# A down projection on two halves of TensorE's array, in a two-layer encoder trunk

## The chip, the cores and the metric

The kernel runs on one core of a Trainium2 chip. A core has TensorE (a 128 x 128 matrix array), VectorE (DVE in the profile), ScalarE (ACT), GpSimd (POOL) and SyncE (SP), which here mostly issues transfers. Matmul results go to eight banks of PSUM, each 128 partitions x 512 float32 values; all other data lie in SBUF, also 128 partitions. The metric is the device time of one execution in microseconds.

## The reference

The input is 512 tokens of width 1024 and 256 memory tokens. Two layers follow each other. Layer 0 mixes tokens by differential attention, layer 1 by chunked gated linear attention; both add a cross-attention into the memory tokens in parallel. After the mixer each layer has a gated MLP with a causal convolution of width 3:

```python
def conv_ffn(h, w_up, conv_w, conv_b, w_down):
    u = h @ w_up                       # 1024 -> 2 x 2816
    c = depthwise_causal_conv(u) + conv_b
    a, g = jnp.split(c, 2, axis=-1)
    return (jax.nn.silu(g) * a) @ w_down   # 2816 -> 1024

for i in range(2):
    h = rms_norm(x, attn_norm[i])
    ...
    x = x + jnp.concatenate([mix, cross], axis=-1) @ w_out[i]
    h = rms_norm(x, ffn_norm[i])
    x = x + conv_ffn(h, w_up[i], conv_w[i], conv_b[i], w_down[i])
```

The case is about the last product, `@ w_down`, in both layers: for each of the 1024 outputs a sum over 2816 hidden values, for 512 tokens.

## The kernel before, in words

The residual stream is held transposed: `xT[k]` holds 128 of the 1024 features on the partitions and the 512 tokens along the free dimension. Every large product is done in three terms to keep float32 precision: each operand is split into a rounded part (`hi`) and the rest (`lo`), both of the rounded type float32r, and hi x hi, hi x lo and lo x hi are summed in PSUM. The function `product` (lines 345 to 352) does this for one output tile: for each 128-feature tile of the input it issues three matmuls (lines 350, 351, 352) whose weights are a 128 x 128 block and whose moving operand is 512 tokens wide. Each matmul is preceded by its own load of weights (PEld in the profile). The projections of the mixers use `gemm` (lines 316 to 342, matmuls at 329 to 331), also in three terms, with the tokens as weights.

The MLP (`ffn`, lines 1113 to 1195) works in two halves of the hidden width, of 6 and 5 blocks of 256. In each half the up products come first, 4 per block, with banks tagged "mm" and "sm" in turn (line 1123); VectorE and ScalarE do the convolution, the gate and the split of the result into `mids`, one pair (hi, lo) for each 128 hidden features, 12 or 10 of them. Then comes the down projection of that half: for each of four pieces of 256 outputs, two banks, "lg" and "tp", take one output tile of 128 each; `product` sums over all `mids`, and `update` (line 1075) adds the bank to `xT` on VectorE. There are two banks of each of the four tags, so that a piece can begin while the piece before is still being added. In the second half of layer 0 `update` also makes the split operands of the next layer (line 310 on VectorE) and the running sum of squares (lines 421 to 426), and the stream is saved to DRAM; in the second half of layer 1 each finished tile goes to the output. The very last tile is added and sent in two halves of 256 tokens, by the queues of SyncE and ScalarE (lines 1185 to 1187).

TensorE's order is the order of the program, written by hand. Weights come in blocks of 128 x 1024 by SyncE's queue, ahead of use; ScalarE rounds each block to `whi` (line 252), VectorE takes the rest to `wlo` (line 255). Behind the down projection of layer 0 stands layer 1's first projection, `gemm` with 272 columns: two of its token blocks take "mm" banks and two "lg" banks, the operands made from the last tiles are used last, and after the first block TensorE sums the squares (line 430).

The attention parts already use matmuls on 64 partitions in plain float32: the logits of differential attention (line 736) and of the memory attention (line 608) alternate between partitions 0 to 63 and 64 to 127, each half with a bank of its own. The memory attention's values (line 646) alternate between two halves of the array's columns.

Of the kernel before, what the change touches and what calls it, by code (L numbers as in the profile page):

```python
# [178 lines left out]
def trunk(ctx, tc, head_d, x_t, mem_t, wpack, cols_a_d, cols_d, conv_d, gate_d, rel_bias, diff_lambda, consts, onehot, out):  # L179
    nc = tc.nc  # L180
    mm = nc.tensor.matmul
    V, A, G = nc.vector, nc.scalar, nc.gpsimd
# [9 lines left out]
    def bank(tag):  # L192
        return ps.tile([128, 512], F32, name=f"ps_{tag}", tag=tag)

    def xtile():
        return xs.tile([128, S], F32, name="xt", tag="xs", bufs=XS)

    def split_tiles(pool=None, tag="xs", bufs=XS):
        pool = pool or xs
        return (pool.tile([128, S], F32R, name=tag + "h", tag=tag, bufs=bufs),  # L200
                pool.tile([128, S], F32R, name=tag + "l", tag=tag, bufs=bufs))
# [4 lines left out]
    def blk(b, w=128):  # L206
        return slice(w * b, w * b + w)
# [13 lines left out]
    def tables(name):  # L221
        tc.keep_in_program_order(A.preload_act_table_set(name))


    def newton(v, y, t):
        V.tensor_mul(t, y, y)
        V.scalar_tensor_tensor(t, t, -0.5, v, op0=ALU.mult, op1=ALU.mult)
        V.scalar_tensor_tensor(y, t, 1.5, y, op0=ALU.add, op1=ALU.mult)
# [65 lines left out]
    def weights(key, by_block=False):  # L294
        i = used[0]
        assert plan[i][0] == key, (plan[i][0], key)
        limit = first_of[i] + WB if by_block else first_of[min(i + 2, len(plan))]
        while done[0] < min(max(limit, first_of[i + 1]), len(order)):
            make_block()
        used[0] += 1  # L300
        parts, made[i] = made[i], None
        return parts
# [5 lines left out]
    def split(hi, lo, src, gain):  # L308
        A.activation(hi, src, AF.Copy, scale=gain)
        V.scalar_tensor_tensor(lo, src, gain, hi.bitcast(F32), op0=ALU.mult, op1=ALU.subtract)  # L310
# [34 lines left out]
    def product(p, parts, n, pairs, ids=None):  # L345
        ids = range(len(parts)) if ids is None else ids
        first, last = (ids[0], ids[-1]) if len(ids) == len(parts) else (0, len(parts) - 1)
        for i in ids:
            (hi, lo), (bh, bl) = parts[i], pairs[i]
            mm(p, hi[:, blk(n)], bh, start=i == first, stop=False)  # L350
            mm(p, hi[:, blk(n)], bl, start=False, stop=False)  # L351
            mm(p, lo[:, blk(n)], bh, start=False, stop=i == last)  # L352


    xT = [None] * KT
# [12 lines left out]
    def col(i, t=cols):  # L368
        return t[:, i:i + 1]

    c_attn = lambda l, k: col(8 * l + k, cols_a)
# [27 lines left out]
    def bias_rows(rs, oh):  # L399
        out = []  # L400
        for tag, c in (("lg", slice(0, 512)), ("tp", slice(512, 640))):
            p = bank(tag)[:, :c.stop - c.start]
            mm(p, rs, oh[:, c], start=True, stop=True)
            out.append(p[:6])
        return out
# [12 lines left out]
    first = [bank("mm"), bank("mm"), bank("sm"), bank("sm")]  # L418

    def squares(src, acc):  # L420
        sq = xtile()
        A.activation(sq, src, AF.Square)
        if acc[0] is not None:
            V.tensor_add(sq, sq, acc[0])
        acc[0] = sq
# [17 lines left out]
    with tc.tile_pool(name="ini", bufs=1) as ip, tc.manual_schedule(engines={E.Activation, E.DVE, E.Pool, E.SP}):  # L443
# [10 lines left out]
        p = bank("tp")  # L454
        for n in (4, 2):
            mm(p[:, :128 * n].rearrange("p (a b) -> p a b", a=n), idle, idle.unsqueeze(1).to_broadcast([128, n, 128]),
               start=True, stop=True)
# [23 lines left out]
        parts, acc, split_w = [], [None], [None]  # L481
# [22 lines left out]
        for k in range(KT):  # L504
# [6 lines left out]
            if k == 5:  # L511
                rows = bias_rows(rs, oh)
# [9 lines left out]
            hi, lo = parts[k]  # L522
# [6 lines left out]
            for b, i, t in todo:  # L529
                xp, w = terms[i]  # L530
                mm(first[b][:, t], xp[:, blk(b)], w[:, t], start=k == 0 and i == 0 and t is not right,
                   stop=k == KT - 1 and i == 2)
# [542 lines left out]
    def update(n, p, gain, acc):  # L1075
        V.tensor_add(xT[n], xT[n], p)
        if gain is None:
            return
        xh[n], xl[n] = split_tiles()
        split(xh[n], xl[n], xT[n], gain(n))  # L1080
        squares(xT[n], acc)
# [31 lines left out]
    def ffn(pool, l, acc):  # L1113
        rB = pool.tile([128, S], F32, name="rB", bufs=1)
        us = [pool.tile([128, S + 128], F32, name=f"u{i}", bufs=1)[:, :S + 2] for i in range(4)]
        for u in us:
            G.memset(u[:, 0:2], 0.0)
        nu = [0]

        def up(parts, n):  # L1120
            i = nu[0]
            nu[0] += 1
            p = bank("mm" if i % 4 < 2 else "sm")
            product(p, parts, n, list(zip(xh, xl)))
            return p, us[i % 4]

        def conv(p, u, j):
            V.tensor_mul(u[:, 2:], p, rB)  # L1128
            c = pool.tile([128, S], F32, name="cvo", bufs=6)
            A.activation(c, u[:, 2:], AF.Identity, scale=cv[l][:, 2, j:j + 1], bias=cv[l][:, 3, j:j + 1])  # L1130
            V.scalar_tensor_tensor(c, u[:, 1:S + 1], cv[l][:, 1, j:j + 1], c, op0=ALU.mult, op1=ALU.add)  # L1131
            V.scalar_tensor_tensor(c, u[:, 0:S], cv[l][:, 0, j:j + 1], c, op0=ALU.mult, op1=ALU.add)
            return c

        def row_scales(sq):
            p = bank("tp")
            (one, _), (hi, lo) = split_tiles(), split_tiles()
            G.memset(one[:, :128].bitcast(F32), 1.0)
            A.copy(hi, sq)
            V.tensor_sub(lo, sq, hi.bitcast(F32))  # L1140
            mm(p, one[:, :128], hi, start=True, stop=False)
            mm(p, one[:, :128], lo, start=False, stop=True)
            v, t = xtile(), xtile()
            A.activation(rB, p, AF.Ln, scale=1.0 / D, bias=eps)
            V.tensor_scalar(v, p, 1.0 / D, EPS, op0=ALU.mult, op1=ALU.add)
            A.activation(rB, rB, AF.Exp, scale=-0.5)
            newton(v, rB, t)

        base = 0
        for half, nq in enumerate(HALVES):  # L1150
            mids = []
            for q in range(base, base + nq):
                wa = weights(("ua", l, q))
                wg = None
                for n in range(2):
                    ua = up(wa, n)
                    wg = wg or weights(("ug", l, q))
                    ug = up(wg, n)
                    if q == 0 and n == 0:
                        row_scales(acc[0])  # L1160
                    ca = conv(*ua, 2 * q + n)
                    cg = conv(*ug, 22 + 2 * q + n)
                    A.activation(cg, cg, AF.Silu)
                    V.tensor_mul(ca, ca, cg)
                    mh, ml = split_tiles() if len(mids) < 5 else split_tiles(pool, "mid", 18)
                    A.copy(mh, ca)
                    V.tensor_sub(ml, ca, mh.bitcast(F32))
                    mids.append((mh, ml))
            last = half == 1
            if last and l == 0:  # L1170
                tables("natural_log_exp_and_others")
            acc2 = [None]
            for c in range(4):
                if last and l == 0 and c == 0:
                    gw = gate_raw[0] = pool.tile([128, S], F32, name="cvo", bufs=6)[:96, :384]
                    G.memset(gw, 0.0)
                    for b in range(3):
                        load(gw[32 * b:32 * b + 17], gate_d)
                pn = bank("lg"), bank("tp")
                parts = weights(("dn", l, base, c))  # L1180
                for n in range(2):
                    product(pn[n], parts, n, mids)
                for n in range(2):
                    if last and l == 1 and c == 3 and n == 1:
                        for t, queue in ((blk(0, S // 2), nc.sync), (blk(1, S // 2), nc.scalar)):
                            V.tensor_add(xT[7][:, t], xT[7][:, t], pn[n][:, t])
                            queue.dma_start(out[7, :, t], xT[7][:, t])
                        continue
                    update(2 * c + n, pn[n], (lambda k: c_attn(1, k)) if last and l == 0 else None, acc2)
                    if last and l == 0:  # L1190
                        nc.sync.dma_start(xres[2 * c + n], xT[2 * c + n])
                    if last and l == 1:
                        nc.sync.dma_start(out[2 * c + n], xT[2 * c + n])
            base += nq
        return acc2
# [87 lines left out]
```

## Time and profile before

| | |
|---|---|
| median of 3 runs | 1165.82 us (1165.61 to 1165.84) |
| the profiled execution's own time | 1165.97 us |
| its span, first to last instruction | 1164.1 us |
| TensorE busy, matmuls | 1159.3 us, 5656 matmuls |
| TensorE busy, loads of weights | 966.6 us, 5656 loads |
| VectorE busy | 750.9 us, 1259 instructions |
| ScalarE busy | 545.5 us, 951 instructions |
| the four stretches of the down projection | 65.28, 54.42, 65.28 and 54.42 us |

In a line of the timeline stand the start in microseconds, the duration, the engine, the line of the kernel and the operation, then output <- inputs, the weights' shape (rows * columns of the array), the moving operand's shape and the count of merged instructions; square brackets give idle time before it and what ended it. In the view of groups by line the last numbers are busy time, mean duration in ns and idle time before. In the view of one line or tile the three numbers are the least, median and longest duration in ns, then the first and last start. In the windows view a line is a stretch with its length and each engine's busy time in it (and count of instructions), the granted clock, the share of the transfer engines' time and GB/s. Matmuls overlap each other: the time from start to start tells their rate, the duration doesn't.

### The profile page before, as it was taken

What the parts mean: (1) busy time and instruction counts of PE and PEld (TensorE: products, weight loads), DVE (VectorE), ACT (ScalarE), POOL (GpSimd) and SP (SyncE); (2) the same over time, 40 slices, a digit from 0 to 9 for tenths busy, and PEclk for the clock granted to TensorE, in tenths of its full rate; (3) what the DMA queues carried; (4) which work ended last, traced back from release to release, by engine and by line L of the source; (5) the groups of instructions that cost most, each with busy time, mean ns of one, the idle gap of its engine ahead of it and who ended that gap; (6) DMA issues with size and microseconds to landing.
All of it is one profiled execution on the core that took longest, in us unless ns stands there. A gap on an engine that the chain in (4) does not pass through costs nothing.

```text
span 1164.1 us, 14796 instructions
## 1 busy us (share of the span) xinstructions
PE 1159.3 (100%) x5656; PEld 966.6 (83%) x5656; DVE 750.9 (64%) x1259; ACT 545.5 (47%) x951; POOL 6.5 (1%) x30
## 2 busy tenths in 40 slices
PE   9999999999999999999999999999999999999998
PEld 7888887888888888888888888988888888888887
DVE  7576778688677326677457637767976733576741
ACT  7676687555344213444337634436543421344420
POOL 0000000000000000000000000000000000000000
PEclk9999999999999999999999999999999999999999
DMA  8422242223223223222341220333332323231221
GB/s 298 162 81 85 77 140 73 72 102 130 76 91 125 83 84 125 73 95 98 121 145 60 99 100 7 114 118 104 105 112 73 108 92 109 90 110 73 91 100 45
DMA packets 39652, 117.76 MB, mean 101 GB/s; under 512 B 4767, under 2 KB 7256, under 8 KB 39582
## 3 DMA queue, kind: packets, MB, share of 16 engines
q1 hardware_dynamic: 39150, 116.44, 29.0%
q8 instruction: 44, 0.72, 0.2%
q10 hardware_dynamic: 432, 0.39, 0.1%
q14 instruction: 26, 0.21, 0.1%
HBM read 112.60 MB, written 4.21 MB: 100 GB/s over the span
## 4 chain that ended last, share of the span: by engine, by line
PE 99%; DMA 0%; ACT 0%; DVE 0%; DVEq 0%; issue 0%
PE ps_mm L350 9%; PE ps_mm L352 9%; PE ps_mm L351 9%; PE ps_sm L352 8%; PE ps_sm L350 8%; PE ps_sm L351 8%; PE ps_mm L329 6%; PE ps_mm L331 6%; PE ps_mm L330 6%; PE ps_tp L352 3%; PE ps_lg L352 3%; PE ps_lg L351 3%; PE ps_tp L351 3%; PE ps_lg L350 3%; PE ps_tp L350 3%; PE ps_tp L219 3%
## 5 line engine op out<-in xcount | busy, mean ns | idle before, releaser
L252 ACT CAST whi<-raw 128x1024 fp32r<-128x1024 f32 (+4 forms) x212 | 207.6, 986 | 247.1 <-PE ps_tp L351 120.9
L255 DVE TENSOR_TENSOR wlo<-raw,whi 128x1024 fp32r<-128x1024 f32 (+4 forms) x212 | 240.4, 1140 | 121.8 <-ACT whi L252 118.6
L350 PE MATMUL ps_mm<-xsh,whi 128*128 128x512 f32 x438 | 171.6, 392 | 0.0
L351 PE MATMUL ps_mm<-xsl,whi 128*128 128x512 f32 x438 | 170.5, 389 | 0.0
L352 PE MATMUL ps_mm<-xsh,wlo 128*128 128x512 f32 x438 | 170.5, 389 | 0.0
L350 PE MATMUL ps_sm<-xsh,whi 128*128 128x512 f32 x378 | 147.0, 389 | 0.0
L351 PE MATMUL ps_sm<-xsl,whi 128*128 128x512 f32 x378 | 147.0, 389 | 0.0
L352 PE MATMUL ps_sm<-xsh,wlo 128*128 128x512 f32 x378 | 147.0, 389 | 0.0
L329 PE MATMUL ps_mm<-whi,xsh 128*128 128x512 f32 (+2 forms) x328 | 126.5, 386 | 0.0
L1130 ACT ACTIVATE cvo<-u,cv 128x512 f32<-128x512 f32 x88 | 71.4, 815 | 112.1 <-DVE u L1128 112.1
L331 PE MATMUL ps_mm<-whi,xsl 128*128 128x512 f32 (+2 forms) x328 | 123.0, 375 | 0.0
L330 PE MATMUL ps_mm<-wlo,xsh 128*128 128x512 f32 (+2 forms) x328 | 122.8, 374 | 0.0
L351 PEld LDWEIGHTS ps_mm<-xsl,whi 128*128 128x128 f32 x438 | 82.3, 188 | 17.2 <-DVE xsl L310 0.4
L352 PEld LDWEIGHTS ps_mm<-xsh,wlo 128*128 128x128 f32 x438 | 82.2, 188 | 17.1
L350 PEld LDWEIGHTS ps_mm<-xsh,whi 128*128 128x128 f32 x438 | 82.2, 188 | 16.9 <-issue 0.3
L1131 DVE SCALAR_TENSOR_TENSOR cvo<-u,cv,cvo 128x512 f32<-128x512 f32 x88 | 65.7, 749 | 36.2 <-ACT cvo L1130 36.0
L351 PEld LDWEIGHTS ps_sm<-xsl,whi 128*128 128x128 f32 x378 | 70.9, 188 | 14.8
L352 PEld LDWEIGHTS ps_sm<-xsh,wlo 128*128 128x128 f32 x378 | 70.9, 188 | 14.7
L350 PEld LDWEIGHTS ps_sm<-xsh,whi 128*128 128x128 f32 x378 | 71.0, 188 | 14.7
L331 PEld LDWEIGHTS ps_mm<-whi,xsl 128*128 128x128 f32 x328 | 61.7, 188 | 11.4
L329 PEld LDWEIGHTS ps_mm<-whi,xsh 128*128 128x128 f32 x328 | 61.7, 188 | 11.0 <-issue 0.7
L330 PEld LDWEIGHTS ps_mm<-wlo,xsh 128*128 128x128 f32 x328 | 61.8, 188 | 10.0
(312 smaller groups left out, 1778.1 us busy)
## 6 DMA issues: line engine op xcount, KB each, us to landing
raw<-in_wpack_dram SPq DMA_DIRECT2D x178, 512.0 KB, 3.5
xt<-in_x_t_dram SPq DMA_DIRECT2D x15, 256.0 KB, 5.4
raw<-in_wpack_dram SPq DMA_DIRECT2D x15, 256.0 KB, 5.1
raw<-in_wpack_dram SPq DMA_DIRECT2D x8, 384.0 KB, 3.4
xres<-xt SPq DMA_DIRECT2D x8, 256.0 KB, 3.6
xt<-xres SPq DMA_DIRECT2D x8, 256.0 KB, 5.4
out_dram<-xt SPq DMA_DIRECT2D x7, 256.0 KB, 2.0
bt<-bias_d SPq DMA_DIRECT2D x6, 256.0 KB, 4.7
```

The costliest lines, as they stand in the source:

```text
L219: nc.tensor.transpose(dst, src, ident[:n, :n])
L252: ins = A.copy(hi[:, c], raw[:, c])
L255: V.tensor_sub(lo[:, c], raw[:, c], hi[:, c].bitcast(F32))
L329: mm(p, sh[k][:, blk(b)], hi, start=k == 0, stop=False)
L330: mm(p, sh[k][:, blk(b)], lo, start=False, stop=False)
L331: mm(p, sl[k][:, blk(b)], hi, start=False, stop=k == KT - 1)
L350: mm(p, hi[:, blk(n)], bh, start=i == first, stop=False)
L351: mm(p, hi[:, blk(n)], bl, start=False, stop=False)
L352: mm(p, lo[:, blk(n)], bh, start=False, stop=i == last)
L1130: A.activation(c, u[:, 2:], AF.Identity, scale=cv[l][:, 2, j:j + 1], bias=cv[l][:, 3, j:j + 1])
L1131: V.scalar_tensor_tensor(c, u[:, 1:S + 1], cv[l][:, 1, j:j + 1], c, op0=ALU.mult, op1=ALU.add)
```

## The change

A second function, `product_rows`, takes the place of `product` in the down projection alone. It takes two banks and, for each matmul that `product` would issue, issues two: one with the partitions 0 to 63 of weights and tokens into the first bank, one with partitions 64 to 127 into the second. The output tile is the sum of both banks. The first output of a piece uses the tags "lg" and "tp", the second "mm" and "sm". VectorE adds the first bank to the tokens in an instruction of its own, and `update` adds the second as before. The very last tile has two additions for each of its two halves.

```diff
+    def product_rows(banks, parts, n, pairs):
+        for i, ((hi, lo), (bh, bl)) in enumerate(zip(parts, pairs)):
+            for w, x, first, last in ((hi, bh, True, False), (hi, bl, False, False), (lo, bh, False, True)):
+                for j, p in enumerate(banks):
+                    rows = blk(j, 64)
+                    mm(p, w[rows, blk(n)], x[rows], start=first and i == 0, stop=last and i == len(parts) - 1)
...
-                pn = bank("lg"), bank("tp")
+                pn = [(bank(a), bank(b)) for a, b in (("lg", "tp"), ("mm", "sm"))]
                 parts = weights(("dn", l, base, c))
                 for n in range(2):
-                    product(pn[n], parts, n, mids)
+                    product_rows(pn[n], parts, n, mids)
                 for n in range(2):
+                    k, (p0, p1) = 2 * c + n, pn[n]
                     if last and l == 1 and c == 3 and n == 1:
                         for t, queue in ((blk(0, S // 2), nc.sync), (blk(1, S // 2), nc.scalar)):
-                            V.tensor_add(xT[7][:, t], xT[7][:, t], pn[n][:, t])
+                            V.tensor_add(xT[7][:, t], xT[7][:, t], p0[:, t])
+                            V.tensor_add(xT[7][:, t], xT[7][:, t], p1[:, t])
                             queue.dma_start(out[7, :, t], xT[7][:, t])
                         continue
-                    update(2 * c + n, pn[n], (lambda k: c_attn(1, k)) if last and l == 0 else None, acc2)
+                    V.tensor_add(xT[k], xT[k], p0)
+                    update(2 * c + n, p1, (lambda k: c_attn(1, k)) if last and l == 0 else None, acc2)
```

## The prediction

> **What bounds the kernel now.** I read the page's top first, then the chain that ended last, then TensorE's own rows by line and, in the down projection, start by start.
>
> ```profile
> span 1164.1 us, 14796 instructions
> PE 1159.3 (100%) x5656; PEld 966.6 (83%) x5656; DVE 750.9 (64%) x1259; ACT 545.5 (47%) x951; POOL 6.5 (1%) x30
> PEclk9999999999999999999999999999999999999999
> PE 99%; DMA 0%; ACT 0%; DVE 0%; DVEq 0%; issue 0%
> ```
>
> TensorE carries 99% of the chain at full granted clock; no other engine is above 64%. So whatever the change does to the spacing of matmuls in the down projection goes into the end one for one. Busy time does not give that spacing, because matmuls overlap. The windows view of the four down stretches (from the first matmul of each to the first one after it) and two neighbours of the timeline do:
>
> ```profile
> 373.24:438.52 65.28, 65.28 (x290) 54.05 (x288) 23.04 (x25) 14.66 (x16) 0.00 (x0) 1.00 0.28 97
> 547.32:601.74 54.42, 54.42 (x242) 45.03 (x240) 27.85 (x37) 22.66 (x30) 2.73 (x6) 1.00 0.38 128
> sum 239.40, PE 239.40 PEld 197.98 DVE 88.85 ACT 60.13 POOL 2.73; mean PE 59.85 PEld 49.49 DVE 22.21 ACT 15.03 POOL 0.68
> ...
> 1040.00 0.39 PE L350 MATMUL ps_sm<-xsh,whi 128*128 128x512 f32 x1
> 1040.00 0.19 PEld L351 LDWEIGHTS ps_sm<-xsl,whi 128*128 128x128 f32 x1
> 1040.22 0.39 PE L351 MATMUL ps_sm<-xsl,whi 128*128 128x512 f32 x1
> ```
>
> By the code a stretch has (12 or 10 token tiles) x 3 terms x 8 outputs = 288 or 240 matmuls, 1056 in the four. 239.40 / 1056 = 0.2267 us from start to start (65.28/288 and 54.42/240 give the same). The 0.39 on a row is the life of one matmul, not its price. The load of the next weights (0.19) begins with the matmul before it and is done inside its 0.227: loads are hidden already.
>
> **The change part by part.** *1. Matmuls.* Each of the 1056 becomes a pair on partitions 0-63 and 64-127, each half streaming the same 512 columns into its own bank. If the halves run one after the other the stage doubles; if together, a pair costs one matmul. The trace has such pairs, in the attention logits (lines 608 and 736: 64 partitions, two banks, halves in turn):
>
> ```profile
> L608 PE MATMUL ps_lg<-kmT,xt x2: 480/480/480, 180.3 to 180.3; 64*128 64x256 f32 x2
> L608 PEld LDWEIGHTS ps_lg<-kmT,xt x4: 183/184/186, 180.3 to 180.4; 64*128 64x128 f32 x4
> ...
> L608 PE MATMUL ps_sm<-kmT,xt x16: 376/376/376, 637.2 to 649.1; 64*128 64x256 f32 x16
> ...
> 635.93 0.39 PE L331 MATMUL ps_mm<-whi,xsl 128*128 128x512 f32 x1
> 636.25 1.13 PE L608 MATMUL ps_lg<-kmT,xt 64*128 64x256 f32 x8
> 637.22 1.03 PE L608 MATMUL ps_sm<-kmT,xt 64*128 64x256 f32 x8
> 637.65 0.60 PE L608 MATMUL ps_sm<-kmT,xt 64*128 64x256 f32 x4
> 638.17 0.50 PE L329 MATMUL ps_mm<-whi,xsh 128*128 128x512 f32 x1
> 638.52 0.40 PE L330 MATMUL ps_mm<-wlo,xsh 128*128 128x512 f32 x1
> ...
> 639.91 0.40 PE L330 MATMUL ps_mm<-wlo,xsh 128*128 128x512 f32 x1
> ```
>
> Two matmuls start in the same tenth of a microsecond and four loads of 183 ns begin within 0.1-0.2: halves do run together, loads too. Four pairs from 637.22 last 1.03 in all, the last two of them from 637.65 on 0.60: two more pairs cost 0.43, one 0.215; with the last matmul's life of 0.376, 1.03 leaves 0.654, which is three periods and the 7 to 9 ns by which the second half starts behind the first. I go on with 0.216. Whether a pair costs what one full matmul of its width costs is seen at 192 columns:
>
> ```profile
> 53.16 0.49 PE L736 MATMUL ps_lg<-kT,qT 64*128 64x192 f32 x4
> L736 PE MATMUL ps_lg<-kT,qT x8: 322/323/427, 52.9 to 53.5; 64*128 64x192 f32 x8
> 707.60 0.82 PE L1030 MATMUL ps_sm<-gv,xt 128*128 128x192 f32 x4
> L1030 PE MATMUL ps_sm<-gv,xt x32: 323/326/355, 707.6 to 761.4; 128*128 128x192 f32 x32
> ```
>
> Two pairs in 0.49 with a last life of 0.323: 0.16 per pair, the lag taken off. Four full ones in 0.82 with 0.326: three periods of 0.165. Equal within the rounding. So a pair is priced like one full matmul, and I take 0.2267 for it: change 0.
>
> Two things keep that open. First, those rows are plain float32, and the down projection runs rounded float32, which streams twice as fast:
>
> ```profile
> 702.00 3.71 PE L646 MATMUL ps_sm<-xt,vm 128*64 128x128 f32 x64
> 732.52 0.28 PE L331 MATMUL ps_mm<-whi,xsl 128*128 128x256 f32 x1
> 738.63 0.28 PE L331 MATMUL ps_mm<-whi,xsl 128*128 128x256 f32 x1
> ```
>
> The first row is plain float32 again, 32 pairs of 128 columns that share the array by its columns: 3.71 - 0.27 (the last life) = 3.44 for 31 periods and a slow first one, 0.110 each; against 0.216 for 256 columns that is 0.83 ns a column. Between the other two lie 51 intervals of rounded float32, 6.11/51 = 0.120 for 256 columns; against 0.2267 for 512 that is 0.417 ns. Two halves at that rate are shown nowhere here. Second, the rounded line leaves 0.2267 - 512 x 0.000417 = 0.013 us per matmul beside the streaming, while the plain pairs leave 0.216 - 256 x 0.00083 = 0.003. If the 13 ns belong to the load of that matmul's own rows, each half keeps them, side by side: 0. If they go as in the plain pairs: -0.0107 each. If each of the two loads costs both halves its 13 ns: +0.0133 each. Bounds of the pair: 0.216 to 0.240, and, if the halves don't run together at this rate, 0.454. I take the middle, since at 192 columns pair and full array agree.
>
> *2. Feeding TensorE.* Four instructions per 0.227 instead of two, 57 ns each. In the row at 702.00 64 matmuls and their 64 loads went by in 3.44 us: 27 ns an instruction. Feeding costs 0.
>
> *3. Changing the division of the array.* It happens at the start of each of the four stretches and the end of three (nothing follows the last). Going in, 635.93 to 636.25 is 0.32 where 0.227 is normal, and the first eight (1.13) last 0.10 longer than the next eight (1.03): 0.19. Coming out, 637.22 to 638.17 is 0.95 for four pairs of 0.216, 0.09 too much; 638.17 to 638.52 is 0.12 too much; 638.52 to 639.91 are six intervals in 1.39 instead of 1.36: 0.24. Sum 4 x 0.19 + 3 x 0.24 = 1.5 us. Below nothing it can't go, since the drain is real in every row; up to 2.5 if rounded float32 settles slowly each time.
>
> *4. VectorE.* 31 more additions of a bank and two more half-bank ones.
>
> ```profile
> L1076 DVE TENSOR_TENSOR xt<-xt,ps_lg x16: 686/689/689, 381.6 to 1153.8; 128x512 f32<-128x512 f32 x16
> 601.74 0.28 PE L329 MATMUL ps_mm<-whi,xsh 128*128 128x272 f32 x1
> 604.00 0.28 PE L329 MATMUL ps_mm<-whi,xsh 128*128 128x272 f32 x1
> 602.62 0.68 DVE L1076 TENSOR_TENSOR xt<-xt,ps_tp 128x512 f32<-128x512 f32 x1
> 605.02 0.68 DVE L424 TENSOR_TENSOR xt<-xt 128x512 f32<-128x512 f32 x1
> 609.27 0.17 PE L430 MATMUL ps_sm<-C,xt 128*128 128x1 f32 x1
> 1160.57 0.75 DVE L1186 TENSOR_TENSOR xt<-xt,ps_tp 128x256 f32<-128x256 f32 x2 [6.11 <-PE ps_tp L352]
> 1161.36 0.35 ACTq L1187 DMA_DIRECT2D out_dram<-xt  x1
> ```
>
> 31 x 0.69 = 21 us of work in stretches where VectorE is busy 23.0 of 65.28 and 27.9 of 54.42 us: covered, 0. The tightest spot inside is the border of the layers: the sum of squares is done at 605.7 and TensorE asks for it at 609.27; one more addition makes it 606.4. If that cover went, each late addition would cost its 0.69. At the very end nothing covers: the two half additions take 0.75 and become four, both output transfers queue behind them: +0.75.
>
> *5. Banks.* The second output now uses mm and sm, which up and the next layer's projection use too. The new wait: the next layer's second token block takes the mm bank that holds half of the last output, 18 matmuls of 0.125 after 601.74, at 604.0; it is free when the addition at 602.62 ends, 603.3. The other banks have one product (6.8 or 8.2 us) of room. Cost 0; the same 0.7 us where that cover fails. No DMA and no queue of SP or POOL is moved.
>
> Sum: 1165.97 (profiled execution, span 1164.1) + 0 + 0 + 1.5 + 0 + 0.75 = 1168.2. The median of the runs is 0.15 below that execution: 1168.1.
>
> **The rivals.** *A, the other side: the 13 ns go.* Pairs at 0.216: 1056 x -0.0107 = -11.3, with the 2.3 above 1156.8. For it: every 64-partition row leaves only 3 ns. Against: so do full-array rows of plain float32 (L1030), so rounding, not halving, seems to bring the 13. It decides from 2.2 ns per pair, which pays parts 3 and 4. The Trainium skill, TensorE: Matmul & The Clock Gate, section "Wait — 56ns, not 53.3ns?", gives 215.7 ns from start to start for 512 columns on a warm array; by it the stage would end at this rival's time, though the full-array rows here, at 226.7, disagree with it before the change.
>
> *B: halves disturb each other.* 0.240 a pair: +14.1 + 2.3 = 1182.2; if only the 7 ns between the halves' starts added: +7.4 + 2.3 = 1175.5. For it: two loads and two streams at twice the column rate ever shown for pairs. Against: the plain pairs add no stagger.
>
> *C: no running together at this rate.* 1056 x 0.227 = +240: 1408. Against: the logits rows. The Trainium skill, same page, section "Measured speedup vs the span model", has four row tiles at 512 columns reach 3.07x instead of 4x; taken over as an estimate, a pair would cost 0.2267 x 4 / 3.07 = 0.295 us and the end +72 us, between B and C; no run here shows four tiles.
>
> **How the numbers follow.** Forecast 0.46, A 0.22, B 0.25, C 0.07. The likeliest's own range is 1166.8 to 1169.8 (switches 1.0 to 2.5 us, a tenth of a nanosecond to a whole one per pair). This kernel's measurement tells 0.2% (2.3 us) from nothing, and the forecast lies just at that bound: of its 0.46 I put 0.28 beyond, as settling can only add, and 0.18 within. Slower 0.28 + 0.25 + 0.07 = 0.60, same 0.18, faster 0.22. The range takes in A below and B above and leaves C out: 1155 to 1184.
>
> **What would show it.** In the profile after: lines of the new product with 64*128 forms, 2112 of them; the down stretches 65.3 and 54.4 us long plus some 0.4 (A: 62.2 and 51.8; B: 69 and 58); two half additions more behind the last matmul. Wrong it would be by another pair period than 0.2267, or by idle TensorE at 604 or 438 (banks).

## The result, and the profile after

The changed kernel takes 1168.07 us (median of 17 runs) against 1165.84 for the kernel before (17 runs): 1.0023 times as long, with a 95% interval of 1.0016 to 1.0031, so 2.7 us longer, between 1.9 and 3.6; the medians are 2.2 apart. In both kernels some runs lie about 2 us above the rest (4 of 17 before, 7 of 17 after), and the rest have medians of 1165.61 and 1167.82, again 2.2 apart. The forecast was 1168.1. That it meets the median to within 0.1 us is luck, since the runs of the changed kernel alone go from 1167.47 to 1171.01; what can be compared with the measurement is the 2.25 us that the prediction adds. The profiled execution has a span of 1166.1 us, 2.0 more than before.

The page of the changed kernel, and its windows view cut as before at the first matmul of each down stretch and the first one after it:

```profile
span 1166.1 us, 16968 instructions
PE 1160.0 (99%) x6712; PEld 965.1 (83%) x6712; DVE 771.5 (66%) x1292; ACT 544.7 (47%) x951; POOL 6.5 (1%) x30
PE 99%; DMA 0%; DVE 0%; ACT 0%; DVEq 0%; issue 0%
...
372.87:438.40 65.53, 65.53 (x578) 53.98 (x577) 27.57 (x31) 14.63 (x16) 0.00 (x0) 1.00 0.32 97
547.45:602.09 54.64, 54.64 (x481) 44.98 (x480) 32.41 (x44) 22.19 (x31) 2.73 (x6) 1.00 0.39 127
```

1056 matmuls more, and the stretches are 65.53 and 54.64 us instead of 65.28 and 54.42. Twice as many matmuls take the same time but for 0.2 us. The timeline at the beginning and the end of the first stretch shows why, and where the 0.2 us per stretch lie:

```profile
372.56 0.39 PE L352 MATMUL ps_sm<-xsh,wlo 128*128 128x512 f32 x1
372.87 0.49 PE L360 MATMUL ps_lg<-xsh,whi 64*128 64x512 f32 x1
372.88 0.49 PE L360 MATMUL ps_tp<-xsh,whi 64*128 64x512 f32 x1
373.21 0.39 PE L360 MATMUL ps_lg<-xsl,whi 64*128 64x512 f32 x1
...
437.63 0.39 PE L360 MATMUL ps_mm<-midh,whi 64*128 64x512 f32 x1
437.63 0.39 PE L360 MATMUL ps_sm<-midh,whi 64*128 64x512 f32 x1
437.85 0.39 PE L360 MATMUL ps_mm<-midl,whi 64*128 64x512 f32 x1
438.08 0.39 PE L360 MATMUL ps_mm<-midh,wlo 64*128 64x512 f32 x1
438.08 0.39 PE L360 MATMUL ps_sm<-midh,wlo 64*128 64x512 f32 x1
438.40 0.50 PE L350 MATMUL ps_mm<-xsh,whi 128*128 128x512 f32 x1
438.73 0.40 PE L351 MATMUL ps_mm<-xsl,whi 128*128 128x512 f32 x1
```

Both halves of a pair start within 0.01 us, and the next pair 0.22 to 0.23 later, as one whole matmul did. Going into the stretch, 372.56 to 372.87 is 0.31 instead of 0.227 and the first pair takes 0.33; coming out, 438.08 to 438.40 is 0.32 and the next interval 0.33. The end, first the last matmul of the kernel before, then the changed kernel:

```profile
1160.15 0.39 PE L352 MATMUL ps_tp<-midh,wlo 128*128 128x512 f32 x1
...
1161.36 0.39 PE L360 MATMUL ps_sm<-midh,wlo 64*128 64x512 f32 x1
1161.78 0.75 DVE L1195 TENSOR_TENSOR xt<-xt,ps_mm 128x256 f32<-128x256 f32 x2 [5.32 <-PE ps_sm L360]
1162.45 0.74 DVE L1196 TENSOR_TENSOR xt<-xt,ps_sm 128x256 f32<-128x256 f32 x2
1163.22 0.36 ACTq L1197 DMA_DIRECT2D out_dram<-xt  x1
```

The last matmul starts 1.21 us later than before, and the span ends 2.0 later: 1.2 on the way, about 0.8 behind the last matmul, where four half additions stand in place of two. This execution came into the first stretch 0.37 us earlier than the one before (372.87 against 373.24), so from there to the last matmul it lost 1.6 us, not 1.2.

### The profile page after: what moved, and what is told of

The parts are those of the page before. It is cut to its first block, busy times and chain, and to the rows that moved or that the text cites. A ratio compares the mean times of both kernels' runs of the same rounds, so it can differ in the third digit from the quotient of the medians.

```text
span 1166.1 us, 16968 instructions
## 1 busy us (share of the span) xinstructions
PE 1160.0 (99%) x6712; PEld 965.1 (83%) x6712; DVE 771.5 (66%) x1292; ACT 544.7 (47%) x951; POOL 6.5 (1%) x30
## 4 chain that ended last, share of the span: by engine, by line
PE 99%; DMA 0%; DVE 0%; ACT 0%; DVEq 0%; issue 0%
PE ps_lg L360 10%; PE ps_mm L360 10%; PE ps_mm L350 9%; PE ps_mm L351 9%; PE ps_mm L352 9%; PE ps_sm L352 8%; PE ps_sm L351 8%; PE ps_sm L350 7%; PE ps_mm L329 6%; PE ps_mm L331 6%; PE ps_mm L330 6%; PE ps_tp L219 3%; PE ps_sm L785 1%; PE ps_lg L744 1%; PE ps_mm L539 1%; PE ps_sm L539 1%
```

## The experiments

My theory: a pair of halves costs what one whole matmul costs, so the change is worth nothing in the stretches; what is lost are seven changes of the array's division (1.5 us) and the additions at the end (0.75). The rivals were A (halving takes 13 ns off each matmul), B (halves disturb each other) and C (halves run one after the other at this rate). e1 to e4, and e8 and e9, are one execution each, beside one of the kernel before at 1165.64 and at 1165.14 us, and are read from their stretches; e5 to e7 have several.

**e1: the halves not in turn.**

```diff
-                for j, p in enumerate(banks):
-                    rows = blk(j, 64)
-                    mm(p, w[rows, blk(n)], x[rows], ...)
+        for j, p in enumerate(banks):
+            rows = blk(j, 64)
+            for i, ((hi, lo), (bh, bl)) in enumerate(zip(parts, pairs)):
+                for w, x, first, last in ...:
+                    mm(p, w[rows, blk(n)], x[rows], ...)
```

> The changed kernel, but each output first runs all its matmuls on partitions 0 to 63 and then all on 64 to 127; the number of matmuls, banks and additions is the same. My theory: halves only run together when neighbours in the program stand on different halves, so each of the 2112 matmuls costs its own 0.227 us: the down stretches double from 240 to 479 us, and the time is 1168 + 239 = 1407 us. Rival: TensorE pairs the halves by itself from its queue, whatever their order: 1168 us. Second rival: a matmul on 64 partitions is shorter by itself: between the two.

Measured: 1362.54 us. The windows view and the timeline where the first output goes over from bank lg (lower half) to bank tp (upper half):

```profile
sum 434.73, PE 434.73 PEld 356.50 DVE 110.96 ACT 59.89 POOL 2.73; mean PE 108.68 PEld 89.12 DVE 27.74 ACT 14.97 POOL 0.68
...
381.06 0.39 PE L360 MATMUL ps_lg<-midl,whi 64*128 64x512 f32 x1
381.29 0.39 PE L360 MATMUL ps_lg<-midh,wlo 64*128 64x512 f32 x1
381.30 0.49 PE L360 MATMUL ps_tp<-xsh,whi 64*128 64x512 f32 x1
381.52 0.39 PE L360 MATMUL ps_lg<-midh,whi 64*128 64x512 f32 x1
381.63 0.39 PE L360 MATMUL ps_tp<-xsl,whi 64*128 64x512 f32 x1
381.75 0.39 PE L360 MATMUL ps_lg<-midl,whi 64*128 64x512 f32 x1
381.97 0.39 PE L360 MATMUL ps_lg<-midh,wlo 64*128 64x512 f32 x1
```

On one half alone matmuls follow each other at 0.227 (381.06 to 381.29): half the partitions, the whole price. So the order of the program is what makes halves free; rival C's price is real when they don't stand in turn. But the four stretches sum to 434.7 and not to 2 x 239.4 = 478.8. The rows show where the 44 us went: the first matmul for tp starts at 381.30, while three for lg, which stand ahead of it in the program, start only at 381.52, 381.75 and 381.97. There are 15 such borders in each of four stretches; 44.1 / 60 = 0.73 us each, three matmuls. TensorE pairs a few out of the program's order, and my expectation, which had it pair none, was 45 us too high. The Trainium skill, TensorE: Matmul & The Clock Gate, section "The mechanism", under "What overlaps and what doesn't", has matmuls start and end strictly in program order; these rows, and the time saved with them, disagree for the starts where the rows of the array differ. The profile shows when a matmul starts, not its place in the compiled program: that this keeps the order of the code is taken for granted here.

**e2 and e3: plain float32, in halves and whole.** e2 changes one line of the changed kernel; e3 does the same to the kernel before.

```diff
-                    mm(p, w[rows, blk(n)], x[rows], ...)
+                    mm(p, w[rows, blk(n)].bitcast(F32), x[rows].bitcast(F32), ...)
```

> The changed kernel with the down projection's operands read as plain float32 instead of rounded float32; everything else the same. If the 13 ns beside the streaming belong to the rounded type, a pair costs 512 x 0.83 + 3 = 428 ns (as the logits pairs do for 256 columns), 1056 x 0.201 = +213 us: 1381 us. If they belong to 512 columns or to this stage, 440 ns a pair: 1393 us.

> The kernel before with the down projection's operands read as plain float32, whole array, no halves. If the rounded type brings the 13 ns: 428 ns a matmul, 1166 + 213 = 1379 us, the same stage length as with halves but for the switches. If halving is what takes the 13 ns away (the reasoning of rival A): 440 ns here against 428 with halves, 1166 + 225 = 1391 us.

Measured: 1835.21 and 1832.62 us, both far above. The first stretch of each in the windows view, e2 then e3, and e2's timeline within it:

```profile
373.22:620.62 247.40, 247.40 (x1153) 111.47 (x1152) 27.54 (x31) 15.18 (x16) 0.00 (x0) 1.00 0.09 28
```

```profile
372.90:619.70 246.80, 246.80 (x577) 109.27 (x576) 22.78 (x25) 14.78 (x16) 0.00 (x0) 1.00 0.09 28
```

```profile
399.94 0.59 PE L360 MATMUL ps_lg<-midl,whi 64*128 64x512 f32 x1
399.94 0.59 PE L360 MATMUL ps_tp<-midl,whi 64*128 64x512 f32 x1
400.37 0.59 PE L360 MATMUL ps_lg<-midl,whi 64*128 64x512 f32 x1
400.37 0.59 PE L360 MATMUL ps_tp<-midl,whi 64*128 64x512 f32 x1
```

Each product of plain float32 is two matmuls in the profile (576 where the code has 288), which my totals left out; the eight rows of line 608 were four products too. Per matmul the expectation holds: 246.80 / 576 = 0.4285 us for 512 columns whole, and in halves 0.43 per pair. That answers the question the runs were made for: without the rounded type only some 2 ns stand beside 512 columns of 0.833 ns, with halves or without. The 13 ns belong to the rounded type, halving doesn't remove them, and rival A's reading of the logits rows falls. Halves are longer by 0.60 us in the first stretch and by 0.61 in the second (206.20 against 205.59), which has a sixth fewer pairs: a loss per stretch, not per pair, and so most likely the change of division, though with rounded operands the same windows grew by only 0.25 and 0.22.

**e4: half as long loads of weights,** in the kernel before.

```diff
-            mm(p, hi[:, blk(n)], bh, ...)
+            mm(p[:64], hi[:, 128 * n:128 * n + 64], bh, ...)
```

> The kernel before, but each matmul of the down projection has only the first 64 of its 128 weight columns, so each load of weights is half as long; the count of matmuls and their 512 tokens are as before. Half of the outputs of the down projection are left out (features 64 to 127 of each tile get no MLP contribution). If the 13 ns beside the streaming come from the length of the load: about 6.5 ns fewer in each of 1056, so -7 us: 1159 us. If they are a fixed price of one rounded matmul: 1166 us.

Measured: 1169.48 us, and the first stretch is longer than before (65.28):

```profile
373.31:439.55 66.24, 66.24 (x290) 38.73 (x288) 22.99 (x25) 14.62 (x16) 0.00 (x0) 1.00 0.31 96
```

66.24 / 288 = 0.230 per matmul. The loads are shorter (38.73 us in place of 54.05) and the matmuls 3 ns slower: none of the 13 ns went with the shorter load. The edit also leaves half of the array's columns idle, so it changes more than the load, and why it costs 3 ns more is open.

**e8 and e9: 256 tokens at a time, in halves and whole.**

```diff
-                for j, p in enumerate(banks):
-                    rows = blk(j, 64)
-                    mm(p, w[rows, blk(n)], x[rows], ...)
+                for t in (blk(0, 256), blk(1, 256)):
+                    for j, p in enumerate(banks):
+                        rows = blk(j, 64)
+                        mm(p[:, t], w[rows, blk(n)], x[rows, t], ...)
```

e9 does the same in the kernel before, on the whole array.

> The changed kernel with each matmul of the down projection cut into two of 256 tokens, so 4224 matmuls in halves. If each half keeps 13 ns per rounded matmul, two pairs of 256 tokens cost 2 x 0.120 = 0.240 us in place of 0.227: 1056 x 0.013 = +14 us, 1182 us. If a half pays the 13 ns only per 512 tokens, or the halves hide it for each other at this size: 0.220 to 0.227, 1161 to 1168 us. If feeding 30 ns an instruction is too much: above 1182 us.

> The kernel before with each matmul of the down projection cut into two of 256 tokens, whole array, for comparison with the halves at 256 tokens. The layer's other products of 256 columns went at 0.120 us: 2 x 0.120 = 0.240, 1056 x 0.013 = +14 us, 1180 us; pair and whole alike but for the 2.3 us of switches and end.

Measured: 1181.65 and 1182.32 us. These two times can't be compared with each other to a microsecond, since e9's execution came into its first stretch 2.9 us later than e8's (375.61 against 372.67). The first stretch of e8, then of e9:

```profile
372.67:441.97 69.30, 69.30 (x1153) 69.16 (x1153) 27.56 (x31) 14.65 (x16) 0.00 (x0) 1.00 0.27 93
```

```profile
375.61:444.73 69.12, 69.12 (x578) 69.11 (x577) 23.04 (x25) 14.60 (x16) 0.00 (x0) 1.00 0.29 92
```

69.12 / 576 = 0.120 per whole matmul and 69.30 / 576 = 0.120 per pair: each rounded matmul has its fixed price, and halves pay it side by side. This speaks against rival B too: twice as many matmuls and loads as in e9, and only 0.18 us more in the stretch. What the fixed price is made of, these runs don't say.

**e5: many more changes of division.** Of the two outputs of a piece the first uses the whole array, the second halves.

```diff
-                pn = [(bank(a), bank(b)) for a, b in (("lg", "tp"), ("mm", "sm"))]
+                pn = [bank("lg"), (bank("mm"), bank("sm"))]
...
-                    product_rows(pn[n], parts, n, mids)
+                    (product_rows if n else product)(pn[n], parts, n, mids)
```

> Of the two outputs of each piece the first runs on the whole array (one bank) and the second on halves (two banks), so the array is divided anew 16 times and joined again 15 times instead of 4 and 3. My theory (0.19 us to divide, 0.24 to join, pairs free): 16 x 0.19 + 15 x 0.24 + 0.75 at the end = 7.4 us over before: 1173.2 us. Rival (the loss is in the pairs, a part of a nanosecond or two each, and the switch costs nothing): half as many pairs, so less than the change: 1167 us.

Measured: 1.0069 of the kernel before (1.0056 to 1.0082), so +8.0 us (6.5 to 9.6). A border inside the first stretch, and the stretch's length:

```profile
373.64:440.74 67.10, 67.10 (x433) 53.28 (x431) 24.84 (x28) 14.71 (x16) 0.00 (x0) 1.00 0.29 95
...
389.99 0.39 PE L360 MATMUL ps_mm<-midh,wlo 64*128 64x512 f32 x1
389.99 0.39 PE L360 MATMUL ps_sm<-midh,wlo 64*128 64x512 f32 x1
390.30 0.50 PE L350 MATMUL ps_lg<-xsh,whi 128*128 128x512 f32 x1
390.30 0.19 PEld L350 LDWEIGHTS ps_lg<-xsh,whi 128*128 128x128 f32 x1 [0.35 <-issue]
390.64 0.40 PE L351 MATMUL ps_lg<-xsl,whi 128*128 128x512 f32 x1
```

Half as many pairs and three times the loss: it is the change of division, not the pair. The rows show both parts of it: the wait ahead of the first whole matmul (389.99 to 390.30, 0.31 where 0.227 is normal), and that matmul's own interval (0.34). Its load of weights starts only with it, at 390.30, where a load otherwise starts one matmul earlier and is hidden. Taking the end's 0.75 off, 8.0 - 0.75 = 7.3 us for 31 changes are 0.23 each, between the 0.19 and 0.24 of the prediction.

**e6: no additions of the first bank.**

```diff
-                            V.tensor_add(xT[7][:, t], xT[7][:, t], p0[:, t])
...
-                    V.tensor_add(xT[k], xT[k], p0)
```

> The changed kernel without VectorE's additions of the first bank: 31 whole ones and the two half ones behind the last matmul are left out, so the contribution of partitions 0 to 63 is missing in the sum. My theory: the 31 are hidden, the two half ones stand at the end: -0.75 us, 1167.3 us; the last matmul starts as late as in the changed kernel. Rival (VectorE's extra 21 us delay banks or weights on the way): the last matmul starts earlier as well, and the time falls to that of before or below, 1165.8 us.

Measured: 1167.53 us, 1.0016 of before (1.0007 to 1.0025). The stretches' sum, with the additions (the changed kernel) and without (e6):

```profile
sum 240.25, PE 240.25 PEld 197.90 DVE 107.08 ACT 59.51 POOL 2.73; mean PE 60.06 PEld 49.48 DVE 26.77 ACT 14.88 POOL 0.68
```

```profile
sum 240.26, PE 240.26 PEld 198.07 DVE 88.88 ACT 60.02 POOL 2.73; mean PE 60.06 PEld 49.52 DVE 22.22 ACT 15.01 POOL 0.68
...
1164.03 0.75 DVE L1195 TENSOR_TENSOR xt<-xt,ps_sm 128x256 f32<-128x256 f32 x2 [6.11 <-PE ps_sm L360]
1164.82 0.35 ACTq L1196 DMA_DIRECT2D out_dram<-xt  x1
```

VectorE does 18 us less there, TensorE's stretches don't move by 0.1 us; what goes is the end. The medians differ by 0.54 us, which the intervals alone could not tell from nothing; the rows can: the second output transfer is issued 0.79 us after the additions begin, against 1163.22 - 1161.78 = 1.44 in the changed kernel, 0.65 apart.

**e7: four quarters of 32 partitions,** four banks per output.

```diff
-                    rows = blk(j, 64)
+                    rows = blk(j, 32)
...
-                pn = [(bank(a), bank(b)) for a, b in (("lg", "tp"), ("mm", "sm"))]
+                pn = [tuple(bank(a) for a in ("lg", "tp", "mm", "sm")) for _ in range(2)]
...
-                    V.tensor_add(xT[k], xT[k], p0)
+                    for p in (p0, p2, p3):
+                        V.tensor_add(xT[k], xT[k], p)
```

> Four quarters of 32 partitions with four banks per output in place of two halves; three additions more per output on VectorE than in the kernel before. My theory carried on: four matmuls together cost one, 0.227; switches as in the change, 1.5 us; at the end six half additions more than before, +2.25: 1165.8 + 3.8 = 1169.6 us. Feeding is then 8 instructions in 0.227, 28 ns each, and the most that the trace before has shown is 27. Rival (feeding or running together ends between two and four): 8 instructions at, say, 35 ns give 0.280 a group, 1056 x 0.053 = +56: 1226 us.

Measured: 1172.55 us, 1.0055 of before (1.0041 to 1.0068), +6.4 us where I had 3.8. First its stretch, then the start of the next layer:

```profile
374.91:440.43 65.52, 65.52 (x1153) 57.77 (x1152) 36.91 (x45) 14.59 (x16) 0.00 (x0) 1.00 0.29 99
...
606.34 0.29 PE L331 MATMUL ps_mm<-whi,xsl 128*128 128x272 f32 x1
608.26 0.40 PE L329 MATMUL ps_mm<-whi,xsh 128*128 128x272 f32 x1 [1.63 <-DVE xt L1201]
...
607.53 0.68 DVE L1201 TENSOR_TENSOR xt<-xt,ps_mm 128x512 f32<-128x512 f32 x1
```

Four matmuls together cost one: the stretch is as long as with halves, fed at 0.227 / 8 = 28 ns an instruction. The extra is a new wait, at the place the prediction named for halves: the second token block of the next layer needs the mm bank, whose addition now stands behind two others and one weight block and ends at 608.2, and TensorE idles 1.63 us. From start to start that is 1.92 where 0.13 is normal, 1.8 lost. With that, 3.8 + 1.8 = 5.6, inside the interval of 4.8 to 7.9.

No run here pointed to a version that beats the kernel before: a pair cost at best what one matmul costs, and what stood around it only added.

## Why the prediction was right, point by point

- *Matmuls, change 0.* Right. Inside a stretch the pairs go at the old period, and rounded float32 at twice the column rate doesn't change that (the rows of the changed kernel; e8 against e9; e7 even with four). The argument, that pair and whole array agreed at 192 columns of plain float32, carried over. The plain rows of line 608 were matmuls of half a product each (e2, e3), which the prediction didn't see; since it compared matmul with matmul, the comparison stands.
- *The rivals* fail by the result itself: a pair costs 0.227, not 0.216 (A), 0.240 (B) or 0.454 (C), nor the 0.295 that was worked out from four row tiles; in e7 four took 65.52 / 288 = 0.2275 together. Why A fails is in e2, e3 and e8: the 13 ns are the rounded matmul's own, and each half keeps them. e1 shows that C's price is paid when the halves don't stand in turn. B's smaller price rested on 7 to 9 ns between the starts of two halves in the logits; the trace has 6 to 7 there and 2 to 5 in the down projection, and they add nothing.
- *Feeding, 0.* Right, with 57 ns an instruction as with 28 (e7).
- *Changing the division, 1.5 us.* Right: the four stretches grew by 240.25 - 239.40 = 0.85 us, and the rest (0.1 going in, ahead of each, and the first intervals after each exit) by 0.8: 1.65 in all. The prediction's sign for it was off: the stretches grew by 0.25, 0.22, 0.25 and 0.13, not by some 0.4, because part of each change lies outside these windows. e5 gives 0.23 for each change.
- *VectorE, 0 and 0.75 at the end.* Right: e6 moves only the end, and by 0.65 in the rows.
- *Banks, 0.* Right, and for the reason given; the changed kernel's addition of that bank began at 602.89 and took 0.68, so it was done 0.9 us ahead of the matmul that needs it (604.45, the 19th after the stretch), and nothing waited:

```profile
602.89 0.68 DVE L1199 TENSOR_TENSOR xt<-xt,ps_mm 128x512 f32<-128x512 f32 x1
604.32 0.29 PE L331 MATMUL ps_mm<-whi,xsl 128*128 128x272 f32 x1
604.45 0.29 PE L329 MATMUL ps_mm<-whi,xsh 128*128 128x272 f32 x1
```

e7 shows what the lost cover costs. The prediction had each late addition cost its 0.69; in e7 two more additions and a weight block in the way made it 1.63 of idle time, 1.8 from start to start.
- *Size against the measurement's bound.* The forecast lay at 0.2% and the measured 0.23% (0.16 to 0.31) does too: the shift is real by its interval, and as small as the sum said. The likeliest's own range, 1166.8 to 1169.8, doesn't come out of its terms, though: 0.75 at the end, 1.0 to 2.5 for the changes and 0.1 to 1 ns a pair give 1167.7 to 1170.1. The result lies in both.

## What to carry to other kernels

Splitting a matmul that fills the array into halves of its partitions bought nothing here, with 512 columns or 256: the halves run together throughout only if they stand in turn in the program, and then cost together what one did, plus about 0.23 us each time the array's division changes, a bank, and an addition. Price such a change by the time from start to start, not by busy time, and look for a matmul of the same form elsewhere in the trace, counting how many instructions one line of code makes there. Then ask which bank comes free last: with more banks in use it is the next product that waits.

## What the runs showed that I had not expected

- TensorE starts matmuls of the other half ahead of three that stand before them in the program (e1), worth 0.73 us at each border.
- A plain float32 product is two matmuls of 0.429 us for 512 columns, 0.858 against 0.227 for the rounded type, nearly four times (e3).
- Weights of 64 columns in place of 128 made a rounded matmul 3 ns slower, not faster (e4).
- The first matmuls of an execution can go at 0.43 us each, and for how long differs from one execution to the next. In e7's profile, then in the changed kernel's, two matmuls in a row each:

```profile
5.70 1.05 PE L539 MATMUL ps_sm<-whi,xsh 128*128 128x512 f32 x2
6.55 1.06 PE L539 MATMUL ps_mm<-wlo,xsh 128*128 128x512 f32 x2
```

```profile
5.52 0.63 PE L539 MATMUL ps_sm<-whi,xsh 128*128 128x512 f32 x2
5.99 0.66 PE L539 MATMUL ps_mm<-wlo,xsh 128*128 128x512 f32 x2
```

0.85 us for two against 0.47. In e7 this lasted some ten matmuls longer, and its first down stretch begins 2.0 us later (374.91 against 372.87), with a granted clock of 1.00 over 4 to 11 us in both profiles; the cause stays open. That is nearly as much as the whole effect of the change, so the place of the loss is better read from stretch to stretch than from two spans.
